# A two-layer hybrid trunk with an expert router: one overflow branch behind the output, state-space tables on one engine

## The chip, the cores and the metric

The kernel runs on one core of a Trainium2 chip. Its engines work side by side, each from its own instruction queue, and wait for each other at semaphores: TensorE (PE) multiplies matrices, VectorE (DVE) and ScalarE (ACT) do element-wise work, GpSimd (POOL) element-wise work and indirect transfers, and SyncE (SP) issues most DMA transfers. The metric is the time of one execution on the device in microseconds (us).

## What is computed

512 tokens of width 1024 in float32 go through two layers. Layer 0 mixes with two groups of heads side by side (a chunked retention with four heads, and a diagonal state-space model, S5), layer 1 with a dilated window attention. Behind each mixer stands a router with 16 experts in four groups: each token takes the best group and the best two of its four experts. A norm ends the program:

```python
def reference(x, ...):
    h = x
    for layer in range(DEPTH):
        hn = rmsnorm(h, mix_norm[layer])
        if layer % 2 == 0:
            mixed = parallel_retention_s5(hn, ...)
        else:
            mixed = dilated_attention(hn, c_w_qkv[i], c_w_out[i])
        h = h + mixed
        h = h + hier_moe(rmsnorm(h, ffn_norm[layer]), ...)
    return rmsnorm(h, final_norm)

def hier_moe(xn, w_group, b_group, w_router, b_router, w_gate, w_up, w_down):
    ...
    gval, gsel = lax.top_k(jax.nn.softmax(glog, axis=-1), 1)
    ...
    top_v, top_i = lax.top_k(elog_sel, TOP_K)
    top_w = jax.nn.softmax(top_v, axis=-1) * gval
    ...
    for g in range(N_GROUPS):
        h = jax.nn.silu(jnp.einsum('td,edf->tef', t, w_gate[g])) * jnp.einsum('td,edf->tef', t, w_up[g])
        out = out + jnp.einsum('tef,efd->td', h * combine[:, g, :, None], w_down[g])
```

Each expert has three matrices of 1024x512 float32, so the two layers read 2 x 16 x 6 MB of expert weights.

## The kernel before

The tokens stand in four chunks of 128 rows (`h`). Float32 products are made in three passes (`mm3`, lines 200 to 203): each operand is split into a rounded high part and the rest (`split_to`, line 198: ACT copies the high part, DVE or POOL subtracts it), and PE multiplies high by high, high by low and low by high. So each weight block costs ACT about 1 us and DVE about 1.2 us beside PE's three matmuls.

Order: `tile_trunk_kernel` is run once as Python and writes out every instruction; a scheduler then orders the instructions of each engine. It moves an instruction ahead of others of its engine where nothing holds it; `tc.issue_after(x)` holds one behind x, and a branch (`tc.If`) is a wall that it does not cross. Transfers wait in the queue of the engine that issues them, so a blocked one on SP holds all later loads.

Layer 0's mixer (`layer0_mix`) norms the chunks (`rms`, root at line 222, scaling at line 231), transposes them (line 194) and multiplies by the input weights. Meanwhile the tables of the state-space part are made by element-wise products of 128x1024: those of lines 492 to 497 twice (once for each half of the channels), those of lines 559 and 560 four times; lines 492 to 494 and 559 run on POOL, the others on DVE. `moe_consts` makes eight small constants of the router on DVE, right behind the norm of the chunks.

An expert layer (`moe`) works with lists: for each expert the rows that chose it are gathered (`gather`, with tables of row numbers from `listed`, lines 1035 to 1038), sent through `gate` and `proj` (the weight splits) and `down`, and added back. An expert has room for 128 rows (an H step) or 64 (an L step). The first three experts are fixed; the other thirteen are sorted by their load (`loads`, `by_load`, lines 1050 to 1076), so that SP must read their numbers into registers (line 1430) before it can issue their loads. Should any list overflow (`top > CAP`), a branch runs `moe_any`, every expert on every row. The branch is at lines 1421 and 1422, between the first gather and the lists; each engine reads `cmax` into a register there and compares. With the inputs here it is never taken. Behind it `table(AF.Silu)` has ACT load the table of its next function (line 180).

## Time and profile before

| | us |
|---|---|
| median of three runs | 1119.96 (1118.29 to 1122.01) |
| the profiled execution | 1119.75 |
| its span, first to last instruction | 1117.9 |
| mean granted PE clock, of full speed | 0.978 |
| PE / DVE / ACT / POOL busy | 1045.4 / 731.2 / 564.3 / 190.8 |
| DMA moved | 277.38 MB, mean 248 GB/s |

A row of a group gives what it did, the time it was busy and, in brackets, how long its engine had stood before it and for what. A "q" behind an engine (PEq, SPq) is its sequencer, which handles branches, register loads and DMA issues; PEld is PE's loading of weights. PE's clock is given as a share of full speed; the engine has two levels, 1.2 and 2.4 GHz, and a stretch between them holds some of both. Line numbers are those of the kernel before.

### The profile page before, as it was taken

What the parts mean: (1) busy time and instruction counts of PE and PEld (TensorE: products, weight loads), DVE (VectorE), ACT (ScalarE), POOL (GpSimd) and SP (SyncE); (2) the same over time, 40 slices, a digit from 0 to 9 for tenths busy, and PEclk for the clock granted to TensorE, in tenths of its full rate; (3) what the DMA queues carried; (4) which work ended last, traced back from release to release, by engine and by line L of the source; (5) the groups of instructions that cost most, each with busy time, mean ns of one, the idle gap of its engine ahead of it and who ended that gap; (6) DMA issues with size and microseconds to landing.
All of it is one profiled execution on the core that took longest, in us unless ns stands there. A gap on an engine that the chain in (4) does not pass through costs nothing. (4 is left out here: it accounts for less than half of the span.)

```text
span 1117.9 us, 15980 instructions
## 1 busy us (share of the span) xinstructions
PE 1045.4 (94%) x5951; PEld 764.9 (68%) x5951; DVE 731.2 (65%) x1265; ACT 564.3 (50%) x852; POOL 190.8 (17%) x120
## 2 busy tenths in 40 slices
PE   5989899999799999999889999999989999999994
PEld 4866677787576756766468878777677676576641
DVE  6978952677897866766372273266669876586734
ACT  5433234424676756654453354353448676575724
POOL 3744110000212222210000000000022121231101
PEclk9999999999899999999989999999979999999998
DMA  8252323269888999999842314224768899999974
GB/s 245 76 151 105 105 79 107 83 244 360 311 313 312 374 393 400 389 367 365 322 184 79 114 38 172 91 76 142 273 247 324 297 391 393 397 384 394 356 301 170
DMA packets 84712, 277.38 MB, mean 248 GB/s; under 512 B 23708, under 2 KB 23892, under 8 KB 68368
## 3 DMA queue, kind: packets, MB, share of 16 engines
q1 hardware_dynamic: 72000, 248.31, 59.6%
q0 software_dynamic: 8016, 16.88, 6.1%
q10 hardware_dynamic: 4608, 11.05, 2.6%
q8 instruction: 51, 0.84, 0.3%
q14 instruction: 37, 0.30, 0.1%
HBM read 262.49 MB, written 24.12 MB: 256 GB/s over the span
## 5 line engine op out<-in xcount | busy, mean ns | idle before, releaser
L202 PE MATMUL acc<-R,R 128*128 128x512 f32 x936 | 377.8, 404 | 5.2 <-DVE R L198 5.0
L201 PE MATMUL acc<-R,R 128*128 128x512 f32 x860 | 350.7, 409 | 7.1 <-ACT R L198 6.0
L203 PE MATMUL acc<-R,R 128*128 128x512 f32 x860 | 342.5, 402 | 2.7 <-DVE R L198 2.7
L198 DVE TENSOR_TENSOR R<-F,R 128x1024 fp32r<-128x1024 f32 (+1 forms) x178 | 213.4, 1217 | 147.4 <-ACT R L198 142.2
L198 ACT CAST R<-F 128x1024 fp32r<-128x1024 f32 (+1 forms) x178 | 182.5, 1041 | 188.2 <-PE acc L203 112.7
L202 PEld LDWEIGHTS acc<-R,R 128*128 128x128 f32 x936 | 179.0, 191 | 49.0 <-DVE R L198 11.2
L201 PEld LDWEIGHTS acc<-R,R 128*128 128x128 f32 x860 | 164.3, 191 | 50.2 <-ACT R L198 11.3
L203 PEld LDWEIGHTS acc<-R,R 128*128 128x128 f32 x860 | 164.4, 191 | 41.0 <-DVE R L198 4.6
L1232 POOL DMA_INDIRECT F<-xnd,idx x30 | 50.7, 1690 | 234.9 <-DVE ws L1043 201.0
L1314 PE MATMUL acc<-F,R 128*64 128x512 f32 x304 | 71.2, 595 | 0.0
L198 DVE TENSOR_TENSOR R<-pb,R 128x512 fp32r<-128x512 f32 x84 | 56.9, 701 | 13.6 <-ACT R L198 13.4
L198 ACT CAST R<-pb 128x512 fp32r<-128x512 f32 x84 | 47.6, 586 | 25.9 <-PE pb L194 19.8
L1386 POOL DMA_INDIRECT hd<-m,idx x20 | 37.3, 1863 | 120.4 <-ACT m L1385 117.4
L927 POOL MEMSET R<- 128x1024 f32 x2 | 1.9, 954 | 302.3 <-PE acc L203 302.3
L198 DVE TENSOR_TENSOR R<-R,R 128x1024 fp32r<-128x1024 f32 x40 | 48.0, 1220 | 6.9 <-ACT R L198 6.8
L1314 PEld LDWEIGHTS acc<-F,R 128*64 128x64 f32 x304 | 22.0, 137 | 43.6 <-issue 42.2
L198 ACT CAST R<-R 128x1024 fp32r<-128x1024 f32 x40 | 41.5, 1049 | 15.3 <-PE acc L203 15.0
L203 PE MATMUL acc<-spare,R 128*128 128x512 f32 x116 | 45.6, 393 | 0.0
L201 PE MATMUL acc<-spare,R 128*128 128x512 f32 x116 | 45.6, 393 | 0.0
L194 PE MATMUL pb<-C,F 128*128 128x128 f32 (+1 forms) x296 | 39.4, 265 | 3.4 <-POOL F L494 3.4
L194 PE MATMUL pb<-C,m 128*128 128x128 f32 (+1 forms) x163 | 27.9, 296 | 13.4 <-DVE m L231 10.2
L194 PEld LDWEIGHTS pb<-C,m 128*128 128x128 f32 (+1 forms) x163 | 20.4, 152 | 27.1 <-DVE m L231 10.3
(384 smaller groups left out, 1431.0 us busy)
## 6 DMA issues: line engine op xcount, KB each, us to landing
F<-in_moe_w_up_dram SPq DMA_DIRECT2D x46, 1024.0 KB, 22.2
F<-in_moe_w_down_dram SPq DMA_DIRECT2D x40, 1024.0 KB, 13.5
F<-in_moe_w_gate_dram SPq DMA_DIRECT2D x38, 1024.0 KB, 21.9
R<-in_moe_w_gate_dram SPq DMA_DIRECT2D x20, 1024.0 KB, 9.0
R<-in_moe_w_down_dram SPq DMA_DIRECT2D x12, 1024.0 KB, 16.0
h<-in_moe_w_down_dram SPq DMA_DIRECT2D x12, 1024.0 KB, 24.0
F<-in_c_w_qkv_dram SPq DMA_DIRECT2D x12, 1024.0 KB, 5.2
F<-in_ab_w_in_dram SPq DMA_DIRECT2D x10, 1024.0 KB, 5.0
```

Of the source, the lines that this page charges most:

```text
L194: PE.transpose(dst, src, ident[:n, :n])
L198: return S.copy(hi, src), eng.tensor_tensor(lo, src, hi.bitcast(F32), op=OP.subtract)
L201: PE.matmul(ps, ah, bh, start=first, stop=False)
L202: PE.matmul(ps, ah, bl, start=False, stop=False)
L203: return PE.matmul(ps, al, bh, start=False, stop=last)
L927: G.memset(q.x0, 0.0)
L1232: rows[e] = G.indirect_dma_start(out=xg[e % 2][0:n], out_offset=None, in_=xnd[:, :], in_offset=bass.IndirectOffsetOnAxis(ap=idx[0:n, e, 0: ...
L1314: m = PE.matmul(ps[LIGHT * i:LIGHT * i + LIGHT], x_[:, 4 * kk + k, :], raw[i][:, k, :], start=kk + k == 0, stop=kk + k == 4, skip_group_ch ...
L1386: G.indirect_dma_start(out=hd[:, :], out_offset=bass.IndirectOffsetOnAxis(ap=idx[:, e, 1:2], axis=0), in_=y[:, :], in_offset=None, bounds_ ...
```

## The change

- The branch inside `moe` is gone. Each layer keeps the maximum of its loads (`most`), and one branch stands behind the last output transfer: where a list overflowed, `everything` runs the whole program once more with `moe_any`. So every engine now jumps, at its very end, over a second copy of the program.
- With the branch go its cast of the maximum, the comparison and the scaling of the weights by `fits`. `loads` and `by_load` are called behind the first expert's gate instead of ahead of the gather; SP's register load of the expert numbers is issued in the loop over the experts, just ahead of the first expert that needs it.
- The POOL products of lines 492 to 494 and 559 go to DVE: ten instructions.
- `moe_consts` is called behind the last split of the product that makes u (`wsplit.lo`) instead of behind the norms.
- In `finish` chunk 1 is normed as chunks 2 and 3 are, by DVE alone (line 231), instead of by ACT (line 1492) and POOL (line 1493).
- `behind_of` is `tc.issue_after` in the main program and nothing in the second copy.

```diff
+    path = SimpleNamespace(any=False)
+
+    def behind_of(ins):
+
+        return nullcontext() if path.any else tc.issue_after(ins)
...
-        with tc.issue_after(scaled[3].ins):
-            moe_consts()
...
+        if not path.any:
+            with behind_of(wsplit.lo.ins):
+                moe_consts()
...
-        G.tensor_tensor(BT[:, 0], b[0], l[0], op=OP.mult)
-        G.tensor_tensor(ta, b[1], l[1], op=OP.mult)
-        G.tensor_tensor(BT[:, 0], BT[:, 0], ta, op=OP.subtract)
+        V.tensor_tensor(BT[:, 0], b[0], l[0], op=OP.mult)
+        V.tensor_tensor(ta, b[1], l[1], op=OP.mult)
+        V.tensor_tensor(BT[:, 0], BT[:, 0], ta, op=OP.subtract)
...
-            G.tensor_tensor(ta, c[0], l[im], op=OP.mult)
+            V.tensor_tensor(ta, c[0], l[im], op=OP.mult)
...
-            loads.last = V.tensor_copy(cmax, cf)
...
-            return cf, bT
+            most.append(cf)
+            return bT
...
-                V.tensor_scalar(wt, wt, fits, None, op0=OP.mult)
...
-                with after(by_load.last.ins) if e == 0 else nullcontext():
-                    gather.last = split_to(xh[:, 4 * i:4 * i + 4], xl[:, 4 * i:4 * i + 4], pt)
+                gather.last = split_to(xh[:, 4 * i:4 * i + 4], xl[:, 4 * i:4 * i + 4], pt)
...
-        cf, bT = loads()
-        perm, row = by_load(bT)
         gather(0)
-        top = nc.values_load(cmax[0:1, 0:1], min_val=0, max_val=T)
-        with tc.If(top > CAP):
-            moe_any(l, weights(), xg[1])
         table(AF.Silu)
         m4r.set([1])
         R[wrs[2]] = typed(wrs[2:], F32R)[0]
         listed(1, range(2))
         fetch(1)
...
-        _, vals = nc.values_load_multi_w_load_instructions(
-            row[0:1, :], engines=(mybir.EngineType.SP,), min_val=0, max_val=NE - 1,
-            skip_runtime_bounds_check_because="sums of one-hot rows: each is one of FIXED to 15, or 0")
-        ids.update(zip(range(FIXED, NE), vals))
         listed(2, range(2))
         fetch(2)
         m2r.set([4, 5])
         hs, silu = gate(0)
         fr.set([[0, 2, 3, 4, 7, 5, 6, 1, 8, 12, 13, 14, 10, 11], [1, 3, 4, 2, 6, 0, 7, 5, 8, 12, 13, 14, 10, 11]][l])
-
-        V.tensor_scalar(cf, cf, CAP + 0.5, None, op0=OP.is_le)
+        perm, row = by_load(loads())
         rest()
-        weights(perm, cf)
+        weights(perm)
...
+            if e + 1 == FIXED:
+                _, vals = nc.values_load_multi_w_load_instructions(
+                    row[0:1, :], engines=(mybir.EngineType.SP,), min_val=0, max_val=NE - 1,
+                    skip_runtime_bounds_check_because="sums of one-hot rows: each is one of FIXED to 15, or 0")
+                ids.update(zip(range(FIXED, NE), vals))
             if e + 1 < NE:
...
-                if c < 2:
+                if c < 1:
...
+    def everything():
+
+        path.any = True
+        del F[12:], scaled[:], recips[:]
+        R[:] = [None if i in (4, 5) else typed([i], F32R)[0] for i in range(9)] + [None]
+        own.spare = cst.tile([128, 1024], F32, tag="spare4", name="spare4")
+        m2r.set(range(6))
+        m4r.set(range(2))
+        load_x(0)
+        moe_any(0, layer0_mix())
...
+        moe_any(1, layer1_mix(xT, layer1_weights()))
+        nc.sync.dma_start(growt, I["final_norm"].partition_broadcast(128))
+        for c in range(NCH):
+            finish(c, m4([128, D], "xn"))
+
+    cmax = sm.tile([128, 1], I32, bufs=1, name="cmax")
+    V.tensor_tensor(cmax, *most, op=OP.max)
+    top = nc.values_load(cmax[0:1, 0:1], min_val=0, max_val=BIG)
+    with tc.If(top > CAP):
+        everything()
```

The scheduler's order changes in more places than the diff. Three of them follow; lines of the changed kernel are some six higher (198 is 204, 1035 is 1040, 1422 is 1524).

ACT at the start of the program, before: its constants' table and the two squares of the first chunk, then the root (line 222).

```order
L180 ACT_TABLE_LOAD
L180 ACTIVATE warm<-eps 128x1
L888 DMA srt<-in_srt_dram 128x81
L215 ACTIVATE m_0_90,ss_111<-F_74 128x512
L215 ACTIVATE m_0_90,ss_114<-F_74 128x512
L222 ACTIVATE rs<-ss_114,ss_111 128x1
```

And now:

```order
L186 ACT_TABLE_LOAD
L186 ACTIVATE warm<-eps 128x1
L895 DMA srt<-in_srt_dram 128x81
L221 ACTIVATE m_0_90,ss_111<-F_74 128x512
L221 ACTIVATE m_0_90,ss_114<-F_74 128x512
L186 ACT_TABLE_LOAD
L186 ACTIVATE warm<-eps 128x1
L228 ACT_TABLE_LOAD
L228 ACTIVATE rs<-ss_114,ss_111 128x1
```

Two table loads and a warming instruction (line 186 is `table`) now stand between the first chunk's squares and its root. In the same way a load of the root's table (line 228) now stands ahead of the first root of layer 1, and two pairs of line 186 instead of one ahead of that.

PE at the head of layer 0's experts, before: the last gathered rows (line 1264), the two products of `by_load`, then the branch.

```order
L1009 MATMUL pb<-M,ones 128x16
L194 MATMUL pb<-C,pos 64x128
L1264 MATMUL acc<-m2w,F_79 128x128 x8
L1071 MATMUL pb<-srt,C 1x13
L1075 MATMUL pb<-srt,m_1_91 128x52
L1421 TENSOR_LOAD cmax
L1422 COMPARE_AND_BRANCH
```

And now, from the same gathered rows:

```order
L1016 MATMUL pb<-M,ones 128x16
L1268 MATMUL acc<-m2w,F_79 128x128 x8
L1040 LDWEIGHTS junk
L1040 MATMUL pb<-tl_102,junk 128x2
L1041 LDWEIGHTS junk
L1041 MATMUL pb<-rc,junk 128x2
```

The lists (lines 1040 and 1041) follow the gathered rows directly; the two products of `by_load` stand 81 rows further down.

DVE in the same place, before: the last instructions of `loads` and `by_load` (lines 1050 to 1076), the splits of the gathered rows and the first weight split (all line 198), then the branch.

```order
L1054 CAST cmax<-cf 128x1
L1067 SCALAR_TENSOR_TENSOR srt<-pb,srt 64x13
L1068 TENSOR_REDUCE srt<-srt 64x1
L1440 TENSOR_SCALAR cf<-cf 128x1
L1069 TENSOR_SCALAR srt<-srt 64x52
L198 TENSOR_TENSOR R_82<-acc,R_82 128x512
L1073 CAST srt<-pb 1x13
L1076 COPY pos<-pb 128x4x13
L198 TENSOR_TENSOR R_82<-acc,R_82 128x512
L198 TENSOR_TENSOR R_84<-R_2390,R_84 128x1024
L1421 TENSOR_LOAD cmax
L1422 COMPARE_AND_BRANCH
```

And now:

```order
L1028 TENSOR_TENSOR junk<-C,pos 128x512
L204 TENSOR_TENSOR R_84<-R_2389,R_84 128x1024
L204 TENSOR_TENSOR R_82<-acc,R_82 128x512
L1043 TENSOR_SCALAR idx<-pb 128x2 x2
L204 TENSOR_TENSOR R_82<-acc,R_82 128x512
L1028 TENSOR_TENSOR m2w<-C,pos 128x512
L204 TENSOR_TENSOR R_85<-R_2389,R_85 128x1024
L1043 TENSOR_SCALAR idx<-pb 128x2
L204 TENSOR_TENSOR R_2423<-R_2390,R_2423 128x1024
L204 TENSOR_TENSOR R_84<-R_2390,R_84 128x1024
L1055 TENSOR_REDUCE cf<-pb 128x1
L1056 TENSOR_SCALAR srt<-pb 128x13
```

The gathered rows and the first weight blocks are split (line 204) before `loads` begins at line 1055, and no branch follows.

## Rows read from the trace of the kernel before

**Rows 1.** The page's first part: busy us (share of the span) and instructions of each engine.

```profile
PE 1045.4 (94%) x5951; PEld 764.9 (68%) x5951; DVE 731.2 (65%) x1265; ACT 564.3 (50%) x852; POOL 190.8 (17%) x120
```

**Rows 2.** Busy us by stage (x: instructions); last, PE's clock, DMA share, GB/s.

```profile
30.00:100.00 70.00, 62.94 (x332) 48.98 (x331) 59.01 (x123) 22.77 (x36) 38.99 (x22) 0.98 0.36 106
281.00:295.00 14.00, 9.87 (x55) 7.51 (x54) 10.85 (x19) 7.10 (x8) 5.08 (x3) 0.76 0.66 221
286.00:294.00 8.00, 7.47 (x28) 5.58 (x28) 6.93 (x10) 2.15 (x3) 5.08 (x3) 0.57 0.85 278
346.00:350.00 4.00, 4.00 (x22) 1.40 (x20) 0.97 (x1) 0.00 (x0) 0.00 (x0) 1.00 0.48 72
360.00:400.00 40.00, 40.00 (x204) 27.14 (x202) 31.43 (x37) 26.13 (x30) 10.93 (x6) 1.00 1.03 377
822.00:836.00 14.00, 10.23 (x57) 7.58 (x55) 10.90 (x19) 7.61 (x10) 5.60 (x3) 0.76 0.58 189
```

**Rows 3.** Line 1422, the branch: duration ns min/median/max, first and last start.

```profile
L1422 ACTq COMPARE_BRANCH  x2: 45/45/45, 281.8 to 822.8; - x2
L1422 PEldq COMPARE_BRANCH  x2: 3368/3408/3447, 281.9 to 822.8; - x2
```

**Rows 4.** PE in order of time behind both branches: start, us, operation, [idle before].

```profile
285.38 0.16 PE L1035 MATMUL pb<-tl,junk 128*128 128x2 bf16 x1 [3.60 <-PEq L1422]
...
826.40 0.16 PE L1035 MATMUL pb<-tl,junk 128*128 128x2 bf16 x1 [3.50 <-PEq L1422]
```

**Rows 5.** DVE in order of time, head of layer 0's experts.

```profile
285.76 0.36 DVE L1038 TENSOR_SCALAR idx<-pb 128x2 int32<-128x2 f32 x2 [2.00 <-PE pb L1036]
...
291.60 2.38 DVE L1088 TENSOR_TENSOR gd<-lg,gm 128x16 f32<-128x16 f32 x1
```

**Rows 6.** SP's queue in order of time, layer 0; last, line 1430's register load.

```profile
271.75 0.45 SPq L1200 DMA_DIRECT2D R<-in_moe_w_down_dram  x1
285.41 0.34 SPq L1282 DMA_DIRECT2D m<-in_moe_w_up_dram  x1
...
291.89 0.36 SPq L1200 DMA_DIRECT2D h<-in_moe_w_up_dram  x1
...
L1430 SPq TENSOR_LOAD <-srt x2: 2682/2686/2690, 288.9 to 830.0; - x2
```

**Rows 7.** ACT in order of time: the first expert's activation in layer 0.

```profile
295.32 0.60 ACT L1307 ACTIVATE m<-acc 128x512 f32<-128x512 f32 x1 [0.33 <-PE acc L203]
```

**Rows 8.** DVE groups by shape, 42 to 53 us: xcount | busy us, mean ns.

```profile
L418 DVE TENSOR_TENSOR growt<-growt,h 128x16 f32<-128x16 f32 x2 | 4.0, 2020 | 0.0
...
L495 DVE TENSOR_TENSOR F<-spare,h 128x1024 f32<-128x1024 f32 x1 | 1.2, 1217 | 0.0
...
L416 DVE TENSOR_TENSOR h<-growt 128x16 f32<-128x16 f32 x1 | 0.2, 164 | 0.0
```

**Rows 9.** DVE in order of time in the first mixer.

```profile
72.08 3.25 DVE L497 TENSOR_TENSOR F<-F,m 128x1024 f32<-128x1024 f32 x1
```

**Rows 10.** PE in order of time in the first mixer.

```profile
74.30 1.42 PE L194 MATMUL pb<-C,F 128*128 128x128 f32 x8 [3.42 <-POOL F L494]
```

**Rows 11.** ACT's first root, a table load, PE's first work of layer 1.

```profile
7.32 0.29 ACT L222 ACTIVATE rs<-ss,ss 128x1 f32<-128x1 f32 x1
...
298.43 1.28 ACT L1097 ACT_TABLE_LOAD   x1
299.72 0.22 ACT L1097 ACTIVATE gd<-gd 128x20 f32<-128x20 f32 x1
...
568.66 1.73 PE L194 MATMUL pb<-C,m 128*128 128x128 f32 x7 [0.85 <-DVE m L231]
```

**Rows 12.** DVE in the last norm; output transfers: KB each, us to landing.

```profile
1109.80 2.54 DVE L231 SCALAR_TENSOR_TENSOR F<-h,rs,growt 128x512 f32<-128x512 f32 x2
...
1112.45 1.42 DVE L231 SCALAR_TENSOR_TENSOR F<-h,rs,growt 128x512 f32<-128x512 f32 x2
...
out_dram<-F SPq DMA_DIRECT2D x4, 256.0 KB, 2.5
```

More of the change, by code (lines that the diff above doesn't have):

```diff
@@ L205 @@
     growt = cst.tile([128, D], F32, name="growt")
-    spare4 = cst.tile([128, 1024], F32, tag="spare4", name="spare4")
+    own = SimpleNamespace(spare=cst.tile([128, 1024], F32, tag="spare4", name="spare4"))
     def rowb(src, eng=nc.scalar):
@@ L224, in rstd @@
         return rs
-    scaled, recips, srts = [], [], []
+    scaled, recips, srts, most = [], [], [], []
     def normed(src, rs, grow, xn, halves=range(2)):
@@ L304, in gemm @@
             split(k2)
-            with tc.issue_after(behind) if behind is not None and k2 == nk // 4 else nullcontext():
+            with behind_of(behind) if behind is not None and k2 == nk // 4 else nullcontext():
                 for b in range(4):
@@ L368, in s5_tables @@
         dt = sm.tile([16, 2], F32, bufs=1, name="s5dt")
-        with tc.issue_after(rms.sqrt.ins):
+        with behind_of(rms.sqrt.ins):
             S.activation(dt, ld, AF.Exp)
@@ L436, in s5_tables @@
         V.tensor_tensor(ci, ci, den, op=OP.mult)
-        Bb = shaped(spare4[:, 0:512], [128, 2, 16, 16])
+        Bb = shaped(own.spare[:, 0:512], [128, 2, 16, 16])
         t3 = m4([128, 2, 16, 16], "t3")
@@ L463, in s5_tables @@
         CTd, Bbd = bd[:, 0], bd[:, 1]
-        CTc = shaped(spare4[:, 512:1024], [128, 2, 16, 16])
+        CTc = shaped(own.spare[:, 512:1024], [128, 2, 16, 16])
         G.memset(F[H1], 0.0)
@@ L521, in s5_rotor @@
         E = shaped(m4s[hf], [128, 2, 512])
-        rt = shaped(spare4[:, 512 * hf:512 * hf + 512], [128, 8, 64])
+        rt = shaped(own.spare[:, 512 * hf:512 * hf + 512], [128, 8, 64])
         sh = [128, 8, 8, 8]
@@ L615, in s5_cross @@
                         q = 4 * o + p4
-                        with tc.issue_after(behind.ins):
+                        with behind_of(behind.ins):
                             PE.matmul(py[32 * p4:32 * p4 + 32, j * 64 + 1:(j + 1) * 64], CL[i][:, j, q, :],
@@ L714, in layer0_mix @@
         s5_scan(*E, 0, X)
-        with tc.issue_after(rot.last.ins):
+        with behind_of(rot.last.ins):
             E = s5_rotor(P, 1)
@@ L772, in layer0_mix @@
         wr_.set([6, 7, 8, 4, 5])
-        with tc.issue_after(fr.load.ins):
+        with behind_of(fr.load.ins):
             params = router_params(0, nc.sync)
@@ L839, in layer1_mix @@
             if hf == 0:
-                with tc.issue_after(fr.load.ins):
+                with behind_of(fr.load.ins):
                     params = router_params(1, nc.sync)
@@ L919, in ranks @@
                 G.tensor_copy(q.oh[:, c], oh)
-            if c == 1:
+            if c == 1 and not path.any:
                 rows0()
@@ L1068, in by_load @@
             V.tensor_reduce(rank, gt, AX.X, OP.add)
-            by_load.last = V.tensor_scalar(P, srt[0:64, 0:4 * NS], rank, None, op0=OP.is_equal)
+            V.tensor_scalar(P, srt[0:64, 0:4 * NS], rank, None, op0=OP.is_equal)
             pi = bank(shape=(1, NS))
@@ L1077, in by_load, with weights @@
             return P, ids
-        def weights(P=None, fits=None):
+        def weights(P=None):
             gl = lg[:, :, 0:4]
@@ L1096, in weights @@
             V.tensor_tensor(dd, m[1], m[0], op=OP.subtract)
-            with tc.issue_after(S.activation(gd, gd, AF.Exp).ins):
+            with behind_of(S.activation(gd, gd, AF.Exp).ins):
                 table(AF.Silu)
@@ L1122, in weights, with moe_any @@
             return wt
-        return idx, cmax, M, E, listed, weights, ws, loads, by_load
-    def moe_any(l, wt, buf):
+        return idx, listed, weights, ws, loads, by_load
+    def moe_any(l, q):
+        wt = route(q)[2]()
+        buf = F[9][:, 1024:2048]
         def piece(src):
@@ L1180, in moe_any @@
                     V.scalar_tensor_tensor(hs, ps[n], wcol[:, c:c + 1], hs, op0=OP.mult, op1=OP.add)
-        for c in range(NCH):
-            nc.sync.dma_start(hds[l][c * 128:(c + 1) * 128, :], h[:, c, :])
     def moe(l, rt, norm, done, then=None):
-        idx, cmax, M, E, listed, weights, ws, loads, by_load = route(rt)
+        idx, listed, weights, ws, loads, by_load = route(rt)
         hd = hds[l]
@@ L1221, in light_x @@
             return v3(X[e][:, 0:8 * LIGHT], 8)
-        after = tc.issue_after
+        after = behind_of
         pe = []
@@ L1293, in proj @@
                 with ExitStack() as st:
-                    for i in (rt.last, rt.sqrt, by_load.last) + (gather.last if k2 else ()) if held else ():
+                    for i in (rt.last, rt.sqrt) + (gather.last if k2 else ()) if held else ():
                         st.enter_context(after(i.ins))
@@ L1500 @@
     moe(1, q, I["final_norm"], finish)
+    def everything():
[7 more added lines that the diff above has]
+        moe_any(0, layer0_mix())
+        nc.sync.dma_start(growt, I["mix_norm"][1].partition_broadcast(128))
+        for i in (4, 5, 6, 7):
+            R[i] = typed([i], F32R)[0]
+        xT = xT_tiles([4, 5, 6, 7])
+        for c in range(NCH):
+            xT_chunk(xT, c, rms(h[:, c, :], growt, m4([128, D], "xn")))
+        moe_any(1, layer1_mix(xT, layer1_weights()))
+        nc.sync.dma_start(growt, I["final_norm"].partition_broadcast(128))
+        for c in range(NCH):
+            finish(c, m4([128, D], "xn"))
[4 more added lines that the diff above has]
+        everything()
 _OUTS = [((1, T, D), "float32")]
```

5 lines of the change are left out of this document (2 added, 3 removed).

## The prediction

> **What bounds the kernel now.** I read the page's first part, then the busy time by stage, then the waits and the order of time at the places that the change touches. TensorE (PE) is busy 1045.4 us of a 1117.9 us span [rows 1], so only two sorts of time can go: the 72.5 us in which PE stands, and the stretches in which its clock is low. The table by stage [rows 2] shows where they are: in the bulk of an expert layer (360 to 400 us) PE is busy 40.00 of 40.00 at clock 1.00 and the DMA share is 1.03, so nothing there is to be had; but in the 14 us at the head of each expert layer (281 to 295, 822 to 836) PE works 9.87 and 10.23 us at a mean clock of 0.76. In the first mixer (30 to 100 us) PE works 62.94 of 70.00, with VectorE (DVE) busy 59.01 and GpSimd (POOL) 38.99.
>
> **The branches inside the two expert layers.** The rows of the branch's line [rows 3] show what it costs each engine: ACT passes it in 45 ns, PE's queue needs 3368 to 3447 ns. The order of PE's work [rows 4] shows the stall: 3.60 us before its next matmul in layer 0, 3.50 us in layer 1, both put down to PE's own queue. Then the clock falls: from 286 to 294 us it is 0.57 of full speed [rows 2], between the two levels of 1.2 and 2.4 GHz. At 0.57 eight microseconds hold what 4.6 would at full clock, so the fall costs up to 3.4 us more. DVE stands too: 2.00 us at 285.76, for PE's list matmuls [rows 5]. And SP issues no load from 271.75 to 285.41 [rows 6], across the branch.
>
> After the change nothing of this stands in the layer: PE goes from the gathered rows to the lists and the gate matmuls. The eleven small DVE instructions of loads and by_load move behind the first expert's splits; at 0.16 us each (the small row in [rows 8]) they are about 1.8 us, and weights() fills part of the room that they leave. The gain per layer is at least the stall, 3.5 us, if the clock falls as before. It is at most the stall and the fall together, some 7 us, or with the odd half microsecond 7.5. Between them stands DVE: it is busy 10.85 of those 14 us [rows 2], of which 2.38 are one small subtraction that waited for a POOL instruction [rows 5], 2.2 more than the small row; run without a hole it would be through some 14 - 10.85 + 2.2 = 5.4 us earlier, and the 1.8 us of list work moved behind it give the rest. I take 6 us for each layer, **-12 us**, between -7 and -15.
>
> What hides the rest: the gain is passed on only if the weight stream comes along. The DMA share is 1.03 from 360 us, but from 346 to 350 it was 0.48 with PE busy 4.00 of 4.00 [rows 2]: the queue had run dry there, since it waits for buffers that PE and the splits give back. So the stream starts its dense part from PE's progress, and when PE is 6 us ahead it starts 6 us earlier. SP also gains: its load at 285.41 can go some 4 us earlier. Against that stands the register load of the expert numbers on SP, 2.69 us [rows 6], which is the same instruction at the same place in SP's queue but now waits for by_load behind the first gate. Behind it stand all loads whose expert is looked up, the first of them at 291.89 before. I work it out to 296: gate(0), whose activation began at 295.32 [rows 7], ends at about 289, the list work is woven into the up splits for 3 to 4 us, then 2.69. So this stretch of the stream begins 4 us later than before while PE is 6 ahead; the dry 4 us at 346 and its like cover it, as I read it. Without that cover it is the rival on the other side below. The scaling by fits, the cast of the maximum and the comparison go with the branch: three small DVE instructions a layer, off PE's path, nothing.
>
> **The state-space tables.** Ten POOL products of 128x1024 go to DVE, where one of that shape takes 1.22 us [rows 8]: +12.2 us of DVE time, and about 1.3 us of router constants (eight instructions at the small row) come into the same stage. What DVE gets back is beside it: two 128x16 instructions between 42 and 53 us took 2.02 us each, where their like take 0.16, with a POOL product running, and the product at 72.08 took 3.25 instead of 1.22 [rows 8, 9]. That is 5.7 us held up in three places, 1.9 for each; seven like places among the ten POOL products give 13 us back for 13.5 taken, three of them only 6. PE's largest wait in this stage is 3.42 us at 74.30, for a POOL product [rows 10]. That wait would turn into one for the same table on DVE, earlier. So the stage can gain at most the 3.42 and the lower clock that follows it, 6 us; and if DVE got nothing back it would have 59.01 + 13.5 = 72.5 us of work for 70 [rows 2], a loss of 2.5, with the order's unevenness 3. I take **-2 us**, since giving and taking nearly cancel and only part of the wait is PE's alone.
>
> **Activation tables.** The block's walls went with the branch, and so the scheduler draws two pairs of table loads to other places. At the start ACT now loads twice and warms once between the first chunk's squares and its root: 2 x 1.28 and a small activation of 0.22, 2.8 us [rows 11], before a root that stood at 7.32. PE's first transposes wait for that norm, but behind them PE waits for splits and further chunks as well, so I pass on about half, **+1.5**, between 0 and 2.8. At the passage to layer 1 the root's table is loaded anew before the first root, and PE's first transposes at 568.66 had waited 0.85 us for that chain [rows 11], so the whole 1.28 lands on PE: **+1.3**, between 0 and 1.3. The pair that stood behind each branch is gone, and I give nothing for it: what DVE waited for there was PE [rows 5].
>
> The Trainium skill weighs these two heavier: "ScalarE: Activation LUTs" (What ACT_TABLE_LOAD costs) has 1283 ns for the load and about 1380 ns more for draining the engine at each switch. The trace has the load at 1.28, but the function behind one starts at 299.72, when the load that began at 298.43 is just over [rows 11]: no drain is seen. By the page the three added loads would cost 4.1 us more and the sum would be 1112.7, inside the forecast's own range.
>
> **The last norm and the branch at the end.** Chunk 1 is normed by DVE instead of ACT and POOL. Before, DVE's two halves of chunk 2 took 2.54 us beside POOL's last products, those of chunk 3 1.42 [rows 12]; POOL will be through with its two earlier, so chunk 2 costs 1.42 and the last half ends 1.1 us earlier, and the reciprocal between them no longer waits: **-1.2**, between 0 and -2.5. The new branch stands behind the last output transfer on SP. ACT, DVE, POOL and PE are through earlier. Each engine now jumps over the whole program written a second time. The trace has only one long price of a jump, PE's 3.4 us [rows 3], and a short one, 45 ns; if SP pays the long one it does so while its last 256 KB are landing, 2.5 us [rows 12], and what remains is about 0.9 and a few semaphores: **+1.3**, between 0 (short, or hidden) and 5 (a second such fetch behind it, partly hidden).
>
> That the price falls on every engine is what the Trainium skill would have: "Runtime: NRT & Kernel Launch" (Instruction fetch mechanics) says that a taken branch to code outside the engine's window waits for a fetch of its target. The rows agree for PE and can't show it for SP, whose jump was short before. By the rule it is the +1.3; if only PE pays, it is 0 and the sum 1107.3.
>
> **Sum**, against the profiled execution's own 1119.75 us (its span and 1.85 around it; the median of the runs is 1119.96, so the two count as one): -12 - 2 + 1.5 + 1.3 - 1.2 + 1.3 = -11.1, that is 1108.6 us.
>
> **Rivals.**
> - Half the gain at the branches: the split chain on ACT and DVE sets gate(0), PE stands between its parts, and the clock falls all the same. For it: DVE's 10.85 of 14 us. Against it: the 2.00 us hole of DVE waited for PE. Gain 3 us a layer instead of 6: 1114.6.
> - DVE becomes the bound of the first mixer. For it: 59.01 of 70 before. Against it: the small instructions held up by POOL. +3 instead of -2: 1113.6.
> - Slower: the expert numbers come too late for the weight stream. SP stands at its register load with all later loads behind it; if the stream has no slack, its dense part begins 4 us later in each layer instead of 6 earlier, and the branches' -12 become +8: 1128.6; with half of it covered by the dry stretches, +4, 1124.6. It decides where PE, between 320 and 400 us, begins to wait for weights. For it: DMA 1.03 in the bulk. Against it: the 0.48 at 346.
> - The change does nothing that counts: a half gain at the heads (-6) meets a mixer a little slower (+1), the table loads (+2.8), the norm (-1.2) and a whole PE-like fetch at the end (+3.4): 1119.75 + 0 = 1119.8.
>
> **Chances.** 0.58 for the forecast (its own range 1103 to 1113), 0.18 and 0.10 for the first two rivals, 0.08 for the slower one, 0.06 for no change. Differences within 0.3% (3.4 us) count as none, about what a measurement of this kernel can tell. The first three cases are faster, less a tail of 0.02 that mixes the mixer's loss with a half gain: 0.84 faster, 0.07 the same, 0.09 slower. The range 1102 to 1117 leaves out the slower case, the no-change case and the ends of the others, about 0.2.
>
> **What would show it.** Right: no stall of PE's queue at 281 and 822; PE's clock near 1.00 or only briefly low there; the first gate's activation some 6 us earlier against the start of the layer; small DVE instructions of 0.16 us in the mixer; two table loads before the first root; and all later landmarks of a layer shifted by the same amount. Wrong: PE waiting for weights after 320 us; clock still 0.76 at the heads; DVE without holes and PE waiting for it between 30 and 100 us; or more than 5 us from the last output instruction to the end.

## The result, and the profile after

The changed kernel takes 1112.84 us (median of 7 runs, 1108.52 to 1117.84), before 1119.96 (7 runs, 1118.29 to 1122.01): ratio 0.9933, 95% interval 0.9914 to 0.9952. The profiled execution took 1111.81 us with a span of 1110.0. So it is 7.1 us faster by the medians, 7.9 by the two spans. The forecast was 11.1. The runs of the changed kernel scatter over 9 us, those of before over 4 here and, in 17 later ones, over 9 as well (1115.58 to 1125.06).

The page's first part of the changed kernel, the line that answers to [rows 1]:

```profile
PE 1038.4 (94%) x5951; PEld 759.2 (68%) x5951; DVE 728.4 (66%) x1272; ACT 565.4 (51%) x852; POOL 163.4 (15%) x108
```

The busy time by stage of the changed kernel (columns as in [rows 2]). The heads of the expert layers now stand at 273 to 287 and 812 to 826:

```profile
30.00:100.00 70.00, 64.71 (x459) 51.61 (x461) 64.87 (x152) 25.34 (x42) 14.98 (x15) 0.98 0.35 106
273.00:287.00 14.00, 10.34 (x73) 8.16 (x72) 13.89 (x28) 10.03 (x14) 5.62 (x4) 1.00 0.61 225
350.00:390.00 40.00, 40.00 (x204) 27.11 (x202) 31.39 (x37) 26.07 (x30) 11.36 (x6) 1.00 1.03 379
812.00:826.00 14.00, 10.98 (x80) 8.37 (x78) 13.71 (x30) 10.54 (x14) 5.66 (x4) 1.00 0.56 199
```

Both heads are at full clock, where they were at 0.76, and DVE is busy 13.89 and 13.71 of 14 us instead of 10.85 and 10.90. The branch's stall is gone. PE is hardly busier for it (10.34 and 10.98 us against 9.87 and 10.23), though at full clock it gets through more in that time: it now waits for DVE. In the window of the mixer POOL fell from 38.99 us to 14.98 and DVE rose from 59.01 to 64.87; the window holds somewhat later work now.

A sum over the whole program says little where gains and losses alternate. The next table follows the same instruction through several kernels: its start in the kernel before, and how much earlier (-) or later (+) it starts in the others. Each is read from the views in order of time. The last three columns are experiments of the next section. The row of line 669 is called the mixer's end below: the tables' part of the mixer is over there, and from there to the experts little changes (-7.18 to -7.72).

| instruction (line of before) | before | changed | tables on POOL | no Silu call | numbers first |
|---|---|---|---|---|---|
| first root (222) | 7.32 | +2.96 | +2.88 | +0.10 | +2.90 |
| first q tile, behind the tables (669) | 121.48 | -7.18 | -2.37 | -7.62 | -8.23 |
| last rows but one of layer 0's mixer (341) | 267.38 | -7.72 | -2.39 | -8.13 | -8.74 |
| third gate of layer 0 (1307) | 331.50 | -10.04 | -6.71 | -11.10 | -9.28 |
| tenth step of layer 0 (1307) | 511.54 | -8.45 | -5.02 | -9.42 | -9.27 |
| last expert of layer 0 (1317) | 548.75 | -8.47 | -5.00 | -10.96 | -10.80 |
| first attention block (813) | 644.41 | -6.22 | -2.67 | -11.02 | -8.73 |
| last rows of layer 1's mixer (341) | 809.60 | -6.47 | -2.93 | -11.28 | -8.97 |
| third gate of layer 1 (1307) | 872.51 | -12.64 | -9.12 | -17.44 | -12.04 |
| last norm (231) | 1112.45 | -13.58 | -10.40 | -18.60 | -13.72 |
| end of the span | 1117.9 | -7.9 | -4.7 | -13.4 | -8.9 |

Down the changed kernel's column: the mixer gives 7.7 us although its first root is 3 us late; the head of layer 0 gives 2.3; 1.6 of it is lost again late in layer 0 and 2.2 at the passage to layer 1; the head of layer 1 gives 6.2; the last norm, with the steps ahead of it, 0.9; and the last step loses 5.7.

Each column is one execution, and traces differ where nothing was changed. Over the five kernels whose heads no edit touches (the changed one and four of the experiments) the head of layer 0 gives 0.7 to 4.3 us, that of layer 1 gives 1.4 to 6.2. The 1.4 is the run without a branch at the end. From 821 to 836 us its row is the first, that of the changed kernel the second:

```profile
821.00:836.00 15.00, 13.86 (x48) 10.45 (x49) 10.25 (x29) 7.60 (x12) 0.96 (x1) 0.54 0.45 167
```

```profile
821.00:836.00 15.00, 11.88 (x63) 8.94 (x62) 14.19 (x32) 11.04 (x16) 4.62 (x3) 1.00 0.45 164
```

So the low clock, 0.54 here, can come back without the branch in the layer, and the 6.2 lies at the favourable end.

**The start.** ACT of the changed kernel in order of time (start, us):

```profile
7.47 1.28 ACT L186 ACT_TABLE_LOAD   x1
...
8.99 1.28 ACT L228 ACT_TABLE_LOAD   x1
10.28 0.29 ACT L228 ACTIVATE rs<-ss,ss 128x1 f32<-128x1 f32 x1
```

The two loads that the order showed are there, and the first root is at 10.28 instead of 7.32 [rows 11].

**The mixer.** DVE's groups of the changed kernel between 42 and 53 us (xcount | busy us, mean ns), against [rows 8]:

```profile
L498 DVE TENSOR_TENSOR F<-spare,h 128x1024 f32<-128x1024 f32 x1 | 1.2, 1215 | 0.0
...
L424 DVE TENSOR_TENSOR growt<-growt,h 128x16 f32<-128x16 f32 x3 | 0.5, 165 | 0.0
```

The 128x16 instructions of this line now take 165 ns, not 2020. The product of line 498, one of the ten, takes 1.2 us.

**The head of layer 0.** DVE, POOL and PE of the changed kernel in order of time:

```profile
280.98 3.07 DVE L1058 TENSOR_TENSOR cf<-cf,srt 128x1 f32<-128x1 f32 x1
...
281.65 2.38 POOL L204 TENSOR_TENSOR R<-F,spare 128x1024 fp32r<-128x1024 f32 x1
...
285.65 0.50 PE L208 MATMUL acc<-R,R 128*128 128x512 f32 x1 [2.94 <-DVE R L204]
```

A maximum of two columns, one element per row, lasts 3.07 us, until POOL's weight split is through (281.65 + 2.38 = 284.03). The Trainium skill ("SBUF — State Buffer", SBUF: two separate sides) has DVE's instructions with two inputs and POOL's share a port that one of them holds for a whole instruction; this row agrees. PE stands 2.94 us for the split that was queued behind it on DVE. This is [rows 5] over again, with another small instruction: list work moved out of the branch's way met POOL's split.

**The passage to layer 1.** ACT and PE of the changed kernel in order of time:

```profile
558.22 1.28 ACT L228 ACT_TABLE_LOAD   x1
559.51 0.29 ACT L228 ACTIVATE rs<-ss,ss 128x1 f32<-128x1 f32 x1
...
562.79 1.45 PE L200 MATMUL pb<-C,m 128*128 128x128 f32 x8 [2.73 <-DVE m L237]
```

And the same stretch by stage (PE, PEld, DVE, ACT, POOL busy, clock, DMA share, GB/s):

```profile
553.00:568.00 15.00, 10.75 (x34) 7.38 (x34) 13.76 (x26) 9.98 (x24) 0.00 (x0) 0.66 0.61 221
```

PE's wait for the first norm is 2.73 us, where it was 0.85 [rows 11], and the stretch runs at clock 0.66.

**The end.** DVE and SP of the changed kernel in order of time:

```profile
1097.25 1.51 DVE L237 SCALAR_TENSOR_TENSOR F<-h,rs,growt 128x512 f32<-128x512 f32 x2
...
1098.87 1.42 DVE L237 SCALAR_TENSOR_TENSOR F<-h,rs,growt 128x512 f32<-128x512 f32 x2
...
1099.54 2.68 SPq L1494 DMA_DIRECT2D out_dram<-F  x4
```

The rows of its branch, line 1524 (columns as in [rows 3]; an event semaphore is the next thing that a queue does behind the compare):

```profile
L1524 SPq EVENT_SEMAPHORE  x8: 17/17/17, 1106.2 to 1106.8; - x8
L1524 PEldq COMPARE_BRANCH  x1: 3737/3737/3737, 1092.3 to 1092.3; - x1
...
L1524 ACTq COMPARE_BRANCH  x1: 50/50/50, 1098.4 to 1098.4; - x1
...
L1524 ACTq EVENT_SEMAPHORE  x1: 17/17/17, 1101.0 to 1101.0; - x1
L1524 SPq COMPARE_BRANCH  x1: 50/50/50, 1102.3 to 1102.3; - x1
```

The semaphores of SP at the end of the program, line 1544, in the same columns, up to 1107.5 us and behind that:

```profile
L1544 SPq EVENT_SEMAPHORE  x2: 28/28/28, 1106.8 to 1106.9; - x2
```

```profile
L1544 SPq EVENT_SEMAPHORE  x11: 17/28/28, 1108.5 to 1109.4; - x11
```

And the only DMA queue that still moves anything from 1104.8 us to the end (packets, MB, share), the one that brings instructions:

```profile
q14 instruction: 2, 0.02, 1.0%
```

DVE is through at 1100.29 (1098.87 + 1.42), 9.7 us before the end; before it was 4.0 (1113.87 to 1117.9, [rows 12]). SP compares at 1102.3, in 50 ns, and its next instruction stands at 1106.2. The price of the jump is that gap and not the compare's own duration; only PE's row shows it as a duration, 3737 ns. ACT's gap is 2.5 us. And SP stands a second time, 1.6 us between its second and third semaphore at line 1544, when no output transfer is left to wait for. All ten traces with the long jump show this second stand, 1.2 to 1.6 us. A packet of the instruction queue falls into it here; that it is a second fetch is likely and not shown.

### The profile page after: what moved, and what is told of

Read it like the earlier page. It is cut to its first block, busy times and chain, and to the rows that moved or that the text cites. A ratio compares the mean times of both kernels' runs of the same rounds, so it can differ in the third digit from the quotient of the medians.

```text
span 1110.0 us, 15933 instructions
## 1 busy us (share of the span) xinstructions
PE 1038.4 (94%) x5951; PEld 759.2 (68%) x5951; DVE 728.4 (66%) x1272; ACT 565.4 (51%) x852; POOL 163.4 (15%) x108
## 5 line engine op out<-in xcount | busy, mean ns | idle before, releaser
L204 DVE TENSOR_TENSOR R<-F,R 128x1024 fp32r<-128x1024 f32 (+1 forms) x178 | 215.7, 1230 | 152.0 <-ACT R L204 146.1
L204 ACT CAST R<-F 128x1024 fp32r<-128x1024 f32 (+1 forms) x178 | 182.7, 1040 | 182.2 <-PE acc L209 103.1
L208 PEld LDWEIGHTS acc<-R,R 128*128 128x128 f32 x936 | 177.2, 189 | 55.3 <-DVE R L204 17.6
L207 PEld LDWEIGHTS acc<-R,R 128*128 128x128 f32 x860 | 162.6, 189 | 51.0 <-ACT R L204 12.6
L209 PEld LDWEIGHTS acc<-R,R 128*128 128x128 f32 x860 | 162.8, 189 | 36.7 <-DVE R L204 2.3
```

The source lines that it names most:

```text
L204: return S.copy(hi, src), eng.tensor_tensor(lo, src, hi.bitcast(F32), op=OP.subtract)
L207: PE.matmul(ps, ah, bh, start=first, stop=False)
L208: PE.matmul(ps, ah, bl, start=False, stop=False)
L209: return PE.matmul(ps, al, bh, start=False, stop=last)
```

## The experiments

All were timed against the kernel before, and differ from the changed kernel by the lines shown (and by what the scheduler makes of them). The intervals of the ratios reach 1.6 to 2.6 us to either side, so that a difference below that settles nothing by itself; the traces say more, each for one execution. No run puts the branch back into the layers with the rest of the change in place: what it cost there is read from the traces alone.

**The state-space tables back on POOL.**

```diff
-        V.tensor_tensor(BT[:, 0], b[0], l[0], op=OP.mult)
+        G.tensor_tensor(BT[:, 0], b[0], l[0], op=OP.mult)
...
-            V.tensor_tensor(ta, c[0], l[im], op=OP.mult)
+            G.tensor_tensor(ta, c[0], l[im], op=OP.mult)
```

> The changed kernel with the ten state-space products back on POOL, all else as changed. Theory A (POOL products held up the small DVE instructions, and their removal gave the first mixer its gain): the mixer loses most of the 10.7 us that it gained between the first root (2.96 late) and the landmark at 126.45 before and 118.73 after; that landmark comes at 124 to 129 us, small 128x16 DVE instructions take 2 us again, and the time is 1118 to 1123 us. Theory B (the gain came from the scheduler's new order, from the router constants moved away, and not from POOL): the landmark stays at 118 to 121 us and the time at 1112 to 1115.

Measured: 1116.05 us (1113.81 to 1118.83), ratio 0.9962 (0.9948 to 0.9977). The expectation's landmark, a later instruction of line 669, comes at 124.05 us, 5.3 later than in the changed kernel (4.8 by the table's row). DVE's group there:

```profile
L424 DVE TENSOR_TENSOR growt<-growt,h 128x16 f32<-128x16 f32 x2 | 4.0, 2022 | 0.0
```

It takes 2022 ns each again. PE at the transposes of the finished table, here and then in the changed kernel:

```profile
71.98 1.56 PE L200 MATMUL pb<-C,F 128*128 128x128 f32 x8 [3.44 <-POOL F L500]
```

```profile
68.64 1.06 PE L200 MATMUL pb<-C,F 128*128 128x128 f32 x8
```

PE's wait of [rows 10] is back, 3.44 us for POOL's product of line 500 (494 before); with the tables on DVE there is none. So theory A holds in that POOL's products are the cause, and for the landmark, at the edge of its range. But most of what PE feels is the wait for a POOL product itself, not the small instructions that it holds up. The total is between the two theories. By the medians 3.2 us of the changed kernel's 7.1 are the tables'.

**The same, without the Silu calls** (the next experiment's edit added).

> The changed kernel without the calls for the Silu table and with the ten state-space products on POOL again. Theory A (POOL's products held up DVE, 5.3 us at the mixer's end in the traces with the calls, whatever the first norm does): 1109.5 to 1112 us against 1105.8, the landmark at 121.48 before only 1.5 to 3.5 us early. Theory B (part of the 5.3 us was the late start meeting POOL): 1106.5 to 1108.5.

Measured: 1113.15 us (1108.90 to 1122.36, 12 runs), ratio 0.9945 (0.9922 to 0.9968); the mixer's end at -4.21 against -7.62. PE's wait for the product, 3.43 us, is there too. By the time theory B is out, but neither number is theory A's: the landmark is earlier than its 1.5 to 3.5, and the total is 7.4 us above the run without the calls alone. The trace gives the tables 3.4 us in the mixer; the rest I can't place. The 4.8 and the 3.4 can't be told apart: five traces with the calls and the tables on DVE differ by 1.1 us at this row (-7.18 to -8.29).

**No Silu table call at the head of the layers.**

```diff
         gather(0)
-        table(AF.Silu)
```

> The changed kernel without the call that has ACT load the Silu table at the head of each expert layer; the weights' own call stays. Theory A (the two pairs of loads drawn forward lie on the path at the start and at the passage to layer 1): the first root is back at 7.3 us instead of 10.3, the landmark of the mixer comes 2 to 3 us earlier, the first norm of layer 1 another 1.3, and the time is 1108 to 1110 us. Theory B (the DVE chain of the mixer starts from the tables' parameters and hides the late first norm, the passage alone counts): 1111 to 1112.5.

Measured: 1105.77 us (1104.26 to 1106.88, 4 runs), ratio 0.9866 (0.9851 to 0.9881): less than either theory had. At the start theory B was right: the root is back (+0.10), and the mixer's end gains only 0.4 us. Silu's table is loaded at the gate in either kernel (line 1310; 284.74 and 823.22 us in the changed one, 281.72 and 818.42 here), so the call saved no load. The passage is more than 1.3 us. PE of this kernel in order of time there:

```profile
557.70 1.94 PE L200 MATMUL pb<-C,m 128*128 128x128 f32 x8 [0.85 <-DVE m L237]
```

And its busy time in the stretch that answers to the one above (2.5 us earlier, as its last expert of layer 0 is), then that of the kernel before:

```profile
550.50:565.50 15.00, 12.11 (x46) 8.57 (x46) 13.36 (x26) 9.70 (x25) 0.00 (x0) 0.77 0.45 169
```

```profile
561.50:576.50 15.00, 12.11 (x45) 8.59 (x46) 13.28 (x26) 9.66 (x25) 0.00 (x0) 0.77 0.44 168
```

PE's wait is 0.85 again, and PE works 12.11 of the 15 us at 0.77, as before, against 10.75 at 0.66. In the table the kernel loses nothing between 548 and 644 us, the changed one 2.25. So it is in every trace: the seven kernels with the call in layer 1 lose 2.1 to 2.6 us there, none of the six without it loses any.

**The call in layer 0 only.**

```diff
         gather(0)
-        table(AF.Silu)
+        if l == 0:
+            table(AF.Silu)
```

> The changed kernel with the call for the Silu table kept in layer 0 (its loads stay ahead of the first root of the program) and left out in layer 1 (nothing is drawn into the passage). It parts the two places of which the run without both calls, 1105.8 us, gave the sum. Theory A (the late first root is hidden, as the landmark at the mixer's end was the same with and without it, and the passage carries all): 1105 to 1107.5 us. Theory B (the start carries about half, through the order of the first splits or PE's clock): 1108 to 1111.

Measured: 1107.42 us (1105.11 to 1112.79), ratio 0.9908 (0.9887 to 0.9930). Theory A: with the first root 2.96 us late as before, the mixer's end stands at -7.71 and the first attention block at -11.33. Of what the calls cost, the passage is the part that the traces place. By the ratios to the kernel before, each timed beside its own, leaving out layer 1's call is worth 2.8 us and both 7.5; by the medians 5.4 and 7.1. That the medians differ by 5.4 us and the passage by 2.3 leaves 3 us: in this trace 0.5 of them stand in the mixer, 0.8 in the head of layer 0 (third gate at -11.32), and 1.5 late in layer 0 (last expert at -11.21). The 1.5 are a stretch of lower clock, 0.89 from 515 to 530 us in the changed kernel and 1.00 here. It does not go with the calls: it is 0.89 in two of the later kernels without them and 1.00 in the one with the constants at their old place, which has both. Whether the calls have a part in the rest is open.

**No branch at the end, and a short body for it.** The first leaves out the branch and the second copy of the program, the second keeps the branch around one transfer.

```diff
-    with tc.If(top > CAP):
-        everything()
...
     with tc.If(top > CAP):
-        everything()
+        nc.sync.dma_start(growt, I["final_norm"].partition_broadcast(128))
```

Without the branch:

> The changed kernel without the branch at the end and without the second copy of the program, so an overflowing list would not be handled. Theory A (behind its last instruction each engine pays a fetch for the long jump, SP some 4 us behind its last transfer): 5 to 6 us less, 1107 to 1108 us, and some 4 us from SP's last issue to the end, where now it is 7.8. Theory B (the price forecast, 1.3 us, the rest of the late end is the transfers' own landing): 1111 to 1112.

With the short body:

> The changed kernel with the branch at the end kept, but with a single transfer as its body in place of the second copy, so that the jump is short; an overflowing list would not be handled. Theory A (the price is the distance of the jump): within 1 us of the run without the branch, 1107 to 1109 us, no gap of 4 us on SP behind the compare; PE's compare under 0.2 us. Theory B (the price is the branch itself, its register load and the waits of each queue at its end): 1111 to 1113, the gap on SP stays.

Measured: 1109.66 us (1107.09 to 1114.11), ratio 0.9902 (0.9882 to 0.9922), without the branch; 1107.74 (1104.24 to 1111.15), ratio 0.9884 (0.9865 to 0.9903), with the short body. The branch's line in the latter:

```profile
L1524 PEldq COMPARE_BRANCH  x1: 223/223/223, 1092.7 to 1092.7; - x1
...
L1524 SPq COMPARE_BRANCH  x1: 50/50/50, 1100.4 to 1100.4; - x1
L1524 SPq EVENT_SEMAPHORE  x1: 17/17/17, 1100.9 to 1100.9; - x1
```

PE's jump takes 223 ns instead of 3737, SP's gap is 0.4 us instead of 3.9. From DVE's end to the end of the span it is 5.1 us without the branch and 5.3 with the short body, against 9.7 (8.4 to 9.7 in the ten traces with the long jump). Theory A: the price goes with the distance, 4.4 us of the end. One thing more differs with the short body: SP's last two output transfers stand behind its branch there (1101.05 and 1101.49 us), so the gap is the cleaner comparison. The total without the branch missed its forecast by 1.7, since its run was behind elsewhere (third gate of layer 1 at -10.19). The Trainium skill ("Runtime: NRT & Kernel Launch", Instruction fetch mechanics) says that a taken branch whose target lies outside the engine's window waits for a fetch of it; the two runs agree, for SP as for PE. Four packets of the instruction queue fall into SP's gap in the changed kernel, from 1102.3 to 1106.2 us:

```profile
q14 instruction: 4, 0.03, 2.1%
```

**No branch at the end, without the Silu calls.**

> The changed kernel without the calls for the Silu table and without the branch at the end and the second copy, so an overflowing list would not be handled. It prices the long jump in a kernel whose runs scatter less. Theory A (the 4 to 4.5 us that the traces show behind SP's last issue): 1101 to 1102.3 us. Theory B (about 3, as the medians with the calls had it): 1102.3 to 1103.5.

Measured: 1104.19 us (1102.53 to 1109.98), ratio 0.9875 (0.9854 to 0.9896). Neither theory: the end is 5.1 us behind DVE's last instruction instead of 9.2, 4.1 less, but this run reached its last norm 1.9 us later than the run with the branch (-16.68 against -18.60). The times can't price the jump, the traces can.

**The last output transfers from ACT** (without the Silu calls).

```diff
-                nc.sync.dma_start(out[0, c * 128:(c + 1) * 128, sl], xn[:, sl])
+                eng = nc.scalar if c == NCH - 1 else nc.sync
+                eng.dma_start(out[0, c * 128:(c + 1) * 128, sl], xn[:, sl])
```

> The changed kernel without the calls for the Silu table, and with the last chunk's two output transfers issued by ACT instead of SP. Theory A (SP's jump, 3.9 us behind its last transfer, is the one on the path; ACT's takes about 2.7 and SP's then runs beside the last norm): 1 to 3 us less than 1105.8, 1103 to 1105. Theory B (what comes last is the landing of the transfers and the end sequence behind it): 1105 to 1106.5.

Measured: 1107.74 us (1103.01 to 1109.67), ratio 0.9895 (0.9872 to 0.9917). The end follows DVE by 8.4 us instead of 9.2, so 0.8 is gained there; the time does not show it. SP's compare comes 1.5 us earlier against DVE's end, at 1096.5, but its gap is 4.6 us now, and ACT's, behind its own transfers, 3.6. No verdict.

**POOL's split of the first expert on DVE**, alone and without the Silu calls.

```diff
-        pool = [(0, "w_up", 3), (1, "w_gate", 3)]
+        pool = [(1, "w_gate", 3)]
```

Alone:

> The changed kernel with the one weight split of expert 0 that POOL makes (the last of w_up) made by DVE instead. Theory A (this POOL instruction holds up a small DVE instruction for 2.3 to 3.1 us, and PE stands 1.8 to 2.9 us for it in the head of each expert layer): no small DVE instruction over 0.5 us between 275 and 290, PE's wait there gone, the head of layer 0 about 2 us shorter and the time 1109 to 1111.5. Theory B (the weight stream sets the later landmarks of the layer in any case): the head is shorter, but the landmark at 511.54 before (503.09 after) is where it was; 1112 to 1113.5.

Without the calls:

> The changed kernel without the call for the Silu table at the head of the layers and with the POOL split of expert 0 on DVE. Without the call alone it was 1105.8. Theory A (the collision with POOL is on the path and independent of the table loads): another 1 to 2.5 us less, 1103 to 1105. Theory B (the weight stream takes it back): 1105 to 1106.5.

Measured: 1114.61 us (1111.32 to 1119.05, 9 runs), ratio 0.9954 (0.9939 to 0.9969), alone; 1105.92 (1105.51 to 1106.96, 4 runs), ratio 0.9880 (0.9865 to 0.9895), without the calls, as fast as without this edit. The held-up instruction is gone, but the head is not shorter. The trace of the first, which took 1118.89 us, 4.3 above its median, goes from -8.12 at the mixer's last rows to -4.84 at the third gate; that of the second gains 2.2 us there, against 3.0 in the run without the calls alone. PE's waits of the first between 268 and 310 us (us in total, times, longest):

```profile
PE acc L209 <- DVE R L204: 2.6, 1, 2.6
PE acc L1263 <- DMA R<-xnd,idx: 2.5, 1, 2.5
PE acc L208 <- DVE R L204: 1.4, 2, 0.8
```

PE waits 2.6 and 1.4 us for DVE's splits instead, as it does in the trace of the second; DVE, busy for 13.89 of 14 us already, has one more to do. The 2.5 us for a gathered transfer are the first trace's own. Theory A falls. That the split's collision and its work weigh the same is how I read it; no run parts them.

Where the collision falls is not fixed. In the kernel without the Silu calls, DVE and PE in order of time show it eight DVE instructions further on, and PE's wait at 1.82:

```profile
281.78 2.34 DVE L1074 TENSOR_SCALAR srt<-srt 64x52 f32<-64x52 f32 x1
...
284.17 0.20 PE L1076 MATMUL pb<-srt,C 64*1 64x13 f32 x2 [1.82 <-DVE srt L1074]
```

**The experts' numbers first.**

```diff
+        perm, row = by_load(loads())
         gather(0)
...
-        perm, row = by_load(loads())
         rest()
```

> The changed kernel with loads and by_load called ahead of the first gather again, as before, but with no branch there. Theory A (the weight stream starts late because SP waits for the expert numbers, and that costs the 1.6 us that layer 0 loses near 490 us, from 10.1 ahead of before to 8.45): the looked-up loads start 4 us or more earlier, the loss near 490 is gone, and the time is 1110.5 to 1112 us although the small instructions stand in the head again. Theory B (the loss near 490 is not from the start of the stream): the head is about 2 us longer and nothing comes back, 1113.5 to 1115.

Measured: 1112.75 us (1110.74 to 1116.50), ratio 0.9946 (0.9930 to 0.9961). SP's queue in the changed kernel, in order of time, with its first looked-up load in the second row:

```profile
277.54 0.33 SPq L1287 DMA_DIRECT2D m2w<-in_moe_w_up_dram  x1
290.73 0.35 SPq L1204 DMA_DIRECT2D h<-in_moe_w_up_dram  x1
```

The same load in this kernel:

```profile
279.75 0.36 SPq L1204 DMA_DIRECT2D h<-in_moe_w_up_dram  x1
```

It is 11 us earlier. PE's wait for DVE between 478 and 500 us in the changed kernel (us in total, times, longest):

```profile
PE acc L208 <- DVE R L204: 1.5, 2, 1.2
```

And in this one:

```profile
PE acc L208 <- DVE R L204: 0.3, 1, 0.3
```

The loss near 490 us is gone (-9.28 at the third gate, -9.27 at the tenth step), as theory A had it; the head gains 1.8 us less (0.5 against 2.3), as theory B had it. The two cancel: the time is that of the changed kernel. Early numbers are one way out of this loss: with POOL's split on DVE it is 0.4 in both traces, at loads from 292.02 and 285.72 us on. What links it to the start of the stream is not shown.

**The router's constants at their old place.**

```diff
+        if not path.any:
+            with behind_of(scaled[3].ins):
+                moe_consts()
         P = s5_tables(*par, *s5_BC())
...
-        if not path.any:
-            with behind_of(wsplit.lo.ins):
-                moe_consts()
```

> The changed kernel with the eight router constants made right behind the norms again. Theory A (moving them was half of the mixer's gain, since there they stood ahead of the first weight splits): the landmark at 121.48 before (114.30 after) comes 3 to 5 us later, 1115.5 to 1118 us. Theory B (they are 1.3 us of DVE time, partly hidden): 0 to 1.5 us later, 1112 to 1114.5.

Measured: 1112.35 us (1109.13 to 1116.98), ratio 0.9940 (0.9919 to 0.9961); the mixer's end 0.3 us later, less than traces of one order differ by there. Theory B.

The best version is the changed kernel without the Silu calls, 1105.77 us: it beats the kernel before by 1.3% and the changed one by 0.6%.

## Why the prediction was right, and where not

The total lay in the range and on the right side, 4 us from the forecast; its terms did not. Three of them missed by about 4 us or more, and the misses nearly cancel: that the total came so near is luck in part.

- **The mixer with its start: forecast -2 and +1.5, measured -7.7.** That POOL's products were in the way was right. Giving and taking did nearly cancel on DVE: in the trace before, eight DVE instructions beside POOL's products last some 13 us longer than their like (an estimate, by the same instructions in the changed kernel), against 12.2 us of added products. The step that failed is the next one, that "only part of the wait is PE's alone": the 3.42 us of [rows 10] went whole, and they are back with the tables on POOL. The tables are 4.8 us of the gain (-2.37 against -7.18), 3.4 by the pair without the Silu calls. The start's +1.5 was nothing: the mixer's end doesn't hang on the first root. Some 2.4 us stay without a cause shown, the constants' 0.3 among them; the new order of the first splits was not tried by itself.
- **The head of layer 1: forecast -6, measured -6.2; that of layer 0: forecast -6, measured -2.3.** The stall went in both, and in this trace the low clock too. The first agreement is luck in part, as the 1.4 of the run without the end branch shows. In layer 0 DVE without holes set PE's pace, as the half-gain rival had it (the fall of the clock, which it had too, did not come), and a small instruction was held up by POOL. I had priced that collision in [rows 5] and then let it vanish with the order.
- **The weight stream** was passed on nearly whole. The first looked-up load went at 290.73 us, 1.2 before its old time and not 4 behind it, where I had worked out 296. Against a layer that began 7.7 earlier it is late all the same: with the numbers first 1.6 us come back in layer 0, a sixth of the 10 us a layer of the slower rival, and are paid for in the head.
- **The passage: forecast +1.3, measured 2.2 in the trace.** I counted the load, and neither the whole of PE's longer wait (2.73 against 0.85) nor the lower clock behind it (0.66 against 0.77).
- **The last norm: forecast -1.2.** Chunk 2's two halves went from 2.54 us to 1.51, -1.0.
- **The end: forecast +1.3, measured +5.7**, of which 4.4 to 4.7 are the jump (9.7 against 5.1 and 5.3); the rest stands without the branch too. SP's price was about right, 3.9 for the 3.4 that I took from PE. The step that failed is the overlap: I let 2.5 us of it pass while the last transfers land. They did land behind it, but the semaphores of the branch and of the end of the program all come after the jump, with the second stand of 1.6 us among them, which I had only at the far end of the term's range. And [rows 3] hid the price, since the compare is not where it shows. Line 1422 on SP in the kernel before:

```profile
L1422 SPq EVENT_SEMAPHORE  x16: 17/17/17, 284.4 to 825.7; - x16
...
L1422 SPq COMPARE_BRANCH  x2: 50/52/53, 281.4 to 822.4; - x2
```

From the compare to the next instruction SP stood 3.0 us there (281.4 to 284.4). So its jump was dear before too, over `moe_any` alone (3.0, against 3.9 over the whole program and 0.4 over one transfer), and the prediction's words that it was short, and that the rows can't show SP's price, do not hold.

## What to carry to other kernels

Read the price of a branch from the gap behind the compare on each engine, by the distance of its jump, and not from the compare. When a wall such as a branch goes, look in the new order for what now crosses it: here table loads that nobody needed there. Taking them out gave 5.5 us between the profiled executions and 7.1 between the medians, of which the traces place 2.2. And when work is moved to a fuller engine, ask which wait of the bottleneck engine ends with the move; the sum of the fuller engine's busy time, which hardly changed here, doesn't tell.

## What the runs showed of the hardware

- A DVE instruction on one element per row can last as long as a POOL product: 3.07 us instead of 0.15, and it is not only sums of two tiles: line 1074, a comparison of one tile against a column, lasted 2.34.
- Executions of one program on this chip scattered by 2.6 to 13 us: 2.6 for the kernel without the Silu calls (4 runs), 4 and 9.5 for the kernel before (7 and 17 runs), 9 for the changed one, 13 for the one with the tables on POOL and without the calls (12 runs). Traces of kernels with nearly one order show low-clock stretches at other places, such as 0.54 and 1.00 from 821 to 836 us. And POOL's split behind its gather starts at its own time (281.65 and 281.52 us in two kernels whose DVE stands eight instructions apart there), so it meets another DVE instruction.
- Behind a jump over a whole program SP stood twice, 3.6 to 4.6 us at the compare and 1.2 to 1.6 us soon after, in all ten traces that have one.
